# Contiguous feature chunks for the gather, and one-hot slots made one group ahead, in two mixture-of-experts layers

## The chip, the cores and the metric

The kernel runs on one core of one Trainium2 chip. The metric is the device time of one execution, in microseconds (us). A core has five engines that run side by side and wait for each other through semaphores: TensorE (PE; its weight loads are shown apart as PEld), VectorE (DVE), ScalarE (ACT), GpSimd (POOL) and SyncE (SP), which issues nearly all DMAs here.

## What is computed

Two blocks in a row over 256 tokens of 1024 features, in fp32. The change touches only the two mixture-of-experts layers of the second block. Each token picks one group of 8 experts out of 8 groups and two experts inside it, 64 experts in all:

```python
def hier_moe(h, w_grp, b_grp, w_exp, b_exp, w1, w3, w2):
    ...
    g_sel = jnp.argmax(g_logits, axis=-1)
    ...
    top_p, top_i = lax.top_k(e_prob, TOP_K_IN_GROUP)
    gate = g_gate * top_p / jnp.sum(top_p, axis=-1, keepdims=True)
    expert = g_sel[:, None] * EXPERTS_PER_GROUP + top_i
    ...
    def expert_block(args):
        xb, e = args
        hb = jax.nn.silu(xb @ w1[e]) * (xb @ w3[e])
        return hb @ w2[e]
    ...
    y = y_rows[dest].astype(jnp.float32) * gate_sorted[:, None]
    out = jnp.zeros((N, D), jnp.float32).at[tok_sorted].add(y)
```

w1 and w3 are 1024 x 256 per expert, w2 is 256 x 1024. Around each such layer stands x = layer_norm(alpha * x + f). All weights of all 64 experts are read in each layer.

## The kernel before

The first part of the program (two attention layers, an MLP each, then latent attention) ends at about 920 us of the span. Then `moe` runs twice, with a pooling mixer between.

**Tokens and slots.** `moe` goes through 16 groups of four experts, each expert with 32 slots, 128 slots a group. Instead of moving rows, it multiplies: `s1` holds for every token and expert the slot number (or none); a comparison with `iota` makes the one-hot matrix G [128 tokens, 2 blocks, 128 slots] (L1397, VectorE). The **gather** (L1406) multiplies chunks of x with G and gives `xg`, 8 feature chunks by 128 slots, in two halves of four chunks. Gg (L1425, VectorE) is G times the gates; its transpose GT (L1429, evicted at L1431) brings the results back to the tokens.

**Layout of x.** x is [128 tokens, 2 blocks, 1024 features] in SBUF. The expert weights are read so that partition p holds features 8p to 8p + 7, so feature chunk k is k, k + 8, k + 16 and so on:

```python
xk = x.rearrange("p b (q k) -> p b k q", k=8)
```

In the gather a chunk `xk[:, b, k]` is the stationary operand: 128 elements with a step of 8.

**A group on TensorE.** `up` (L1444): 64 matmuls with w1 and w3, 32 columns an expert, four experts in four column strips. ScalarE takes the tanh (L1448), VectorE makes th and h (L1449, L1451). Then `gather(g + 1)`; `back(g + 1)`, the transposes of Gg; `down(g)`: h is transposed (L1459, evicted at L1461), 32 matmuls with w2 (L1470), the eviction to Y (L1474, L1475) and the way back with GT into the sum (L1479). Then `up(g + 1)`. In this program an fp32 matmul leaves two records in the trace, so `up` shows as 128 and a gather as 32. The first seven gathers of a layer are evicted with gain and shift in eight pieces (L1412, L1414); at group GAIN = 6 `affine` (L1068) applies gain and shift to x itself, and alpha times x is added to the sum (L1586). After group OVER = 8 a branch on the device (L1525) handles experts with more than 32 rows; here it is not taken.

**The weights.** They are streamed through a ring of 21 tiles of [128, 2048] fp32, 1.0486 MB each: 10 from a pool that the first part also uses and 11 more. `raw_w(i)` also issues the DMA of item i + 20 (L180, on SP); SP waits there until the tile's earlier user is done. A group takes 8 items of w1 and w3, in pairs, and 4 of w2. The items of the second layer follow those of the first without a break.

**What sets the order.** The schedule is manual: every engine runs its instructions in the order in which the program writes them. PSUM tiles of the experts come in turn from four banks.

Of the kernel before, what the change touches and what calls it, by code (L numbers as in the profile page):

```python
# [70 lines left out]
def _layout(inputs):  # L71
    """The arrays of the launch: the inputs, the small vectors also laid end to end, constants of the shapes."""
    a = {n: np.ascontiguousarray(inputs[n]) for n in _INS}
    a["rows"] = np.concatenate([a[n].reshape(-1, 128) for n in _ROWS])
    a["brows"] = np.concatenate([a[n].reshape(-1, 128) for n in _BROWS])
    a["wr"] = np.concatenate([a["moe_w_grp_2"], a["moe_w_exp_2"]], -1)
    a["br"] = np.concatenate([a["moe_b_grp_2"], a["moe_b_exp_2"]], -1)
    a["cst"], a["poolm"] = _constants()
    return a


class Kern:
# [6 lines left out]
    # ---------------------------------------------------------------- weights  # L89
# [181 lines left out]
    def g_tok(self, xT, key, outs, n, splitn=1, mid=None):  # L271
        """outs[blk][j]: [128, n]: token rows, from both halves of K."""
# [18 lines left out]
    def g_feat(self, xT, key, mid=None, bank=None, end=None):  # L291
        """[128 features, 2, 256 tokens] twice, for 512 features."""
# [73 lines left out]
    def rsqrt(self, r, n):  # L366
        """r <- r ** -0.5 for r [128, n], n <= 4: a seed from the exponent, then Newton steps."""
# [57 lines left out]
    # ---------------------------------------------------------------- attention over pairs of 64-wide heads  # L425
    def attend(self, ap, pairs, scores, V, mask, outp, yts, sink=None, pre=None):
        """Softmax attention, two heads at a time, three pairs in flight. Gives the prologue and the rest."""
# [69 lines left out]
        def main(pend=None, nxt=None, ahead=1):  # L497
            """The pairs in turn; then the products out of the last are still owed. nxt() makes an attention to go on with."""
# [29 lines left out]
    # ---------------------------------------------------------------- mixer 0  # L528
    def mixer0(self):
        nc, A = self.nc, self.A  # L530
        with ExitStack() as st:
# [30 lines left out]
            def lru():  # L562
                col = self.col
                # halves of the biases, 2 * softplus(-lambda)
# [5 lines left out]
                for hf in range(2):  # L570
# [26 lines left out]
                    # tanh(z/2) = w, z = -log a: a = 2/(1+w) - 1, sqrt(1-a^2) = 2 sqrt(w)/(1+w)  # L597
# [34 lines left out]
            def forget():  # L632
                # log sigmoid, running sums, biases
# [72 lines left out]
    def pair_scores(self, qT, kT):  # L706
        """Heads 2p and 2p+1 in the two halves of the partitions of chunk p."""
# [145 lines left out]
    # ---------------------------------------------------------------- squared relu mlp  # L853
# [35 lines left out]
    # ---------------------------------------------------------------- mixer 1  # L889
    def mixer1(self, xT):  # L890
        nc, A = self.nc, self.A
        x = self.x
        with ExitStack() as st:
# [4 lines left out]
            tab = ap.tile([128, 2, 2, 2, 32], F32, name="tab")     # q or k, block, cos or sin  # L898
# [11 lines left out]
            def rope(dst, src, nh, qk, b):  # L910
                """dst, src [128, nh, 64]."""
# [11 lines left out]
            def feat(dst, tk, nch):  # L923
                """tokens x features (two blocks) to features x tokens."""
# [79 lines left out]
    # ---------------------------------------------------------------- rows broadcast to all partitions, layer norm  # L1004
    def bc(self, i, bank=None, mat=None, more=None):
        """row i of brow (times mat's diagonal) on every partition, in two banks; more: rows to add."""
# [10 lines left out]
    def stats(self, y):  # L1017
        """mean and 1 / sqrt(var + eps) of a block of rows in parts, in steps: a seed from the exponent, Newton steps."""
# [23 lines left out]
    def both(self, gens):  # L1042
        """the generators' steps in turn; what they return."""
# [11 lines left out]
    def normed(self, y, dst):  # L1055
        """dst <- (y - mean) / sqrt(var + eps); y[block][half]."""
# [5 lines left out]
    def affine(self, g, bb):  # L1062
        """x <- x * g + b."""
        for o, v in ((ALU.mult, g), (ALU.add, bb)):
            for h in range(2):
                for b in range(2):
                    t = self.x[:, b, h * 512:(h + 1) * 512]
                    self.nc.vector.tensor_tensor(t, t, v[h], op=o)  # L1068

    def router(self, rp):  # L1070
        """the router's weights times the gain of the norm before, less the mean over the rows; its bias plus that of
        the norm's shift. In steps."""
# [22 lines left out]
    def rotary(self):  # L1095
        """tables from the positions: cos, sin [128, block, 16], in steps."""
# [33 lines left out]
    # ---------------------------------------------------------------- latent attention  # L1130
    def mla(self):
        nc, A = self.nc, self.A
        x = self.x
        with ExitStack() as st:
# [33 lines left out]
            # what dies first comes first: the experts' weights follow into it  # L1168
# [97 lines left out]
            # the residual's own norm  # L1266
# [16 lines left out]
    def warm(self, n):  # L1283
        """products that nothing reads, against the drop of TensorE's clock in a wait."""
# [4 lines left out]
    # ---------------------------------------------------------------- experts  # L1289
    def moe(self, l, wp, bank, y, before_last):  # L1290
        """x becomes the norm's output before gain and shift, of y[block][half]; bank: banks that are free at the start.
        The sum is returned. The router's weights are free of their columns' means, so that it can take y as it is."""
# [8 lines left out]
        # logits, token rows; feature chunk k is k, k + 8, ...  # L1301
        xk = x.rearrange("p b (q k) -> p b k q", k=8)
# [4 lines left out]
        for b in range(2):  # L1307
            for h in range(2):
                nc.scalar.activation(x[:, b, h * 512:(h + 1) * 512], y[b][h], AF.Copy)
# [18 lines left out]
        def one_hots(v, n, k):  # L1328
            """the first k of v [128, 2, 8] from the largest on, the first of equals first: one-hot, and values."""
# [32 lines left out]
        def gates():  # L1362
            nonlocal gt, ci
            # gates
# [18 lines left out]
            # further rounds of 32 rows an expert  # L1383
# [10 lines left out]
        def gather(g, s, first=False):  # L1394
            """rows of group g: [128 features, 8, 128 slots], in halves of the features, and the one-hot slots."""
            G = wp.tile([128, 2, 4, 32], F32, name="G", bufs=1)
            tt(G, s[:, :, 4 * g:4 * g + 4, None].to_broadcast([128, 2, 4, 32]),  # L1397
               iota[:, None, None, :].to_broadcast([128, 2, 4, 32]), op=ALU.is_equal)
            Gf = G.rearrange("p b e s -> p b (e s)")
# [20 lines left out]
            return xg, G, half  # L1420

        def back(g, G):
            """the weighted way back [128 slots, 256]."""
            Gg = wp.tile([128, 2, 4, 32], F32, name="Gg", bufs=1)
            tt(Gg, G, gt[:, :, 4 * g:4 * g + 4, None].to_broadcast([128, 2, 4, 32]), op=ALU.mult)  # L1425
# [8 lines left out]
        def up(g, xg, parts, mid=None, fill=()):  # L1434
            """fill: work of others to go between the parts."""
# [18 lines left out]

        def down(g, h, GT, acc, getw2, first, end, fill=()):
            """fill: where the last products are left, if it isn't empty."""
# [4 lines left out]
            nc.scalar.activation(hT, ps, AF.Copy)  # L1461
            if getw2 is None:
# [24 lines left out]
        def last(g, hT, GT, acc):  # L1487
            """the same for the last group, whose weights come in quarters of the columns."""
# [31 lines left out]
        def overflow():  # L1520
            """the experts with more than 32 rows."""
# [3 lines left out]
            with self.tc.If(more > 0):  # L1525
                with self.tc.For_i(0, more, 1):
# [22 lines left out]
                    for g in range(16):  # L1549
                        xg, G, half = gather(g, s2)  # L1550
                        half(1)
                        GT = back(g, G)
                        h = up(g, xg, parts2(g))
                        down(g, h, GT, acc, lambda: getw2(g), False, False)

        xg, G, half = gather(0, s1, True)
        h = up(0, xg, parts(0), lambda: (gates(), half(1)))
        GT = back(0, G)
        acc = self.pacc()
        for g in range(16):  # L1560
            this = h, GT
            w2g = lambda: [((0, 1), [(e, w2(l, g, e)) for e in range(4)])]
            if g == OVER:
                down(g, *this, acc, w2g, False, False)
                overflow()
            if g == GAIN:
                self.affine(self.bc(2 * l), self.bc(4 + 2 * l))
            if g < 15:
                xg, G, half = gather(g + 1, s1, g < GAIN)
                if g:  # L1570
                    half(1)
                    GT = back(g + 1, G)
# [5 lines left out]
            if g != OVER:  # L1578
                down(g, *this, acc, None if (l, g) == (1, 15) else w2g, g == 0, g == 15, fill)
            if g == 0:  # L1580
                half(1)
                GT = back(1, G)
            if g == GAIN:
                for b in range(2):
                    for hf in range(2):
                        nc.tensor.matmul(acc[b][hf], self.alpha_id, x[:, b, hf * 512:(hf + 1) * 512], start=False, stop=False,  # L1586
                                         skip_group_check=True)
            if g < 15:
                h = up(g + 1, xg, parts(g + 1), fill=fill)
        return acc  # L1590

    # ---------------------------------------------------------------- pooling mixer
# [216 lines left out]
```

## Time and profile before

| | us |
|---|---|
| runs of the kernel (device time) | 1928.67, 1929.14, 1932.13; median 1929.14 |
| profiled execution, span from first to last instruction | 1926.0 |
| start of the first expert gather in the span | 920.4 |
| start of the second layer's first gather | 1432.7 |
| end of the last product | 1913.5 |

Start of the reading: the span is one execution, and the device time contains a little around it; the median lies 3.1 us above the span. In the lists, "idle before" is the time for which an engine stood still before an instruction, and behind the arrow stands what ended it. PE records are pipelined and overlap, so their busy time adds up to more than the span they cover. [...] The DMA share is the mean busy share of the core's 16 DMA engines.

### The profile page before, as it was taken

How to read it: one execution, taken by the hardware profiler on the slowest of the kernel's cores; microseconds unless marked ns; L12 is line 12 of the kernel's file. 1: busy time of each engine (PE TensorE's matmuls, PEld its weight loads, DVE VectorE, ACT ScalarE, POOL GpSimd, SP SyncE). 2: the span in 40 equal slices, each digit the busy share in tenths (PEclk: the TensorE clock that was granted, in tenths of full speed). 3: DMA queues.
4: the chain of work that ended last, by engine and by line, in shares of the span. 5: the costliest groups of instructions: out<-in, count | busy, mean ns of one | idle time of the engine just before them, and what ended most of it. 6: DMA issues, size and time to landing. Idle time of an engine off the chain costs nothing. (4 is left out here: it accounts for less than half of the span.)

```text
span 1926.0 us, 29923 instructions
## 1 busy us (share of the span) xinstructions
PE 1748.4 (91%) x12712; PEld 1316.9 (68%) x12712; DVE 749.8 (39%) x1599; ACT 578.8 (30%) x1047; POOL 11.3 (1%) x22
## 2 busy tenths in 40 slices
PE   7999999999999999999888897888998878878886
PEld 7998899989878899877554554555475455545554
DVE  6886576556675655585210111101151111110112
ACT  5644445444564544466111100000021110000001
POOL 0000000000000000000000000000000000000000
PEclk9999999999999999999888889888998879898898
DMA  8544355554524455556899999999989999999993
GB/s 278 179 152 150 117 170 197 187 184 155 196 66 153 147 195 184 177 213 256 341 356 411 415 384 403 409 419 422 418 360 359 378 415 412 386 406 413 422 421 115
DMA packets 160611, 550.11 MB, mean 286 GB/s; under 512 B 9660, under 2 KB 33551, under 8 KB 144463
## 3 DMA queue, kind: packets, MB, share of 16 engines
q1 hardware_dynamic: 158175, 539.18, 73.2%
q0 software_dynamic: 2144, 8.66, 1.2%
q8 instruction: 104, 1.70, 0.3%
q14 instruction: 44, 0.36, 0.0%
q10 hardware_dynamic: 144, 0.21, 0.0%
HBM read 546.97 MB, written 1.05 MB: 285 GB/s over the span
## 5 line engine op out<-in xcount | busy, mean ns | idle before, releaser
L237 DVE TENSOR_TENSOR wl<-wr,wh 128x1024 fp32r<-128x1024 f32 (+4 forms) x268 | 309.5, 1197 | 119.7 <-ACT wh L234 76.1
L1406 PE MATMUL b<-G,x 128*128 128x128 f32 x1024 | 252.5, 418 | 64.6 <-DVE G L1397 64.5
L1406 PEld LDWEIGHTS b<-G,x 128*128 128x128 f32 x1024 | 247.0, 335 | 78.7 <-issue 78.0
L234 ACT ACTIVATE wh<-wr 128x1024 fp32r<-128x1024 f32 (+4 forms) x268 | 265.1, 1037 | 103.9 <-DVE wl L237 72.3
L1444 PE MATMUL b<-wr,xg 128*32 128x256 f32 x4096 | 235.6, 388 | 2.3 <-ACT xg L1414 2.3
L1444 PEld LDWEIGHTS b<-wr,xg 128*32 128x32 f32 x4096 | 129.6, 112 | 113.1 <-issue 28.0
L1470 PE MATMUL b<-wr,hT 128*32 128x512 f32 x992 | 160.6, 806 | 18.0 <-ACT hT L1461 18.0
L320 PE MATMUL a<-wh,yh 128*128 128x512 f32 x416 | 168.0, 404 | 2.7 <-ACT yh L334 2.7
L320 PE MATMUL a<-wh,yl 128*128 128x512 f32 x416 | 165.1, 397 | 0.6 <-DVE yl L335 0.6
L320 PE MATMUL a<-wl,yh 128*128 128x512 f32 x416 | 164.1, 394 | 0.0
L1449 DVE SCALAR_TENSOR_TENSOR th<-th,b 128x256 f32<-128x256 f32 x32 | 13.5, 421 | 326.4 <-ACT th L1448 326.4
L304 PE MATMUL b<-xh,wl 128*128 128x256 f32 x448 | 121.9, 282 | 0.0
L304 PE MATMUL b<-xh,wh 128*128 128x256 f32 x448 | 121.7, 281 | 0.0
L1470 PEld LDWEIGHTS b<-wr,hT 128*32 128x32 f32 x992 | 36.3, 143 | 124.8 <-issue 96.2
L1479 PE MATMUL a<-Y,GT 128*128 128x512 f32 x248 | 118.2, 618 | 0.0
L1448 ACT ACTIVATE th<-b 128x256 f32<-128x256 f32 x32 | 12.3, 384 | 326.9 <-PE b L1444 326.9
L304 PE MATMUL b<-xl,wh 128*128 128x256 f32 x448 | 110.3, 282 | 0.0
L1475 DVE COPY Y<-b 128x512 f32<-128x512 f32 x31 | 21.4, 692 | 206.9 <-PE b L1470 206.9
L320 PEld LDWEIGHTS a<-wh,yh 128*128 128x128 f32 x416 | 78.1, 188 | 23.3 <-ACT yh L334 4.5
L1479 PEld LDWEIGHTS a<-Y,GT 128*128 128x128 f32 x248 | 42.0, 189 | 75.7 <-issue 30.5
L320 PEld LDWEIGHTS a<-wh,yl 128*128 128x128 f32 x416 | 78.1, 188 | 22.5 <-DVE yl L335 3.9
L304 PE MATMUL a<-xh,wh 128*128 128x256 f32 x320 | 90.0, 290 | 1.5 <-ACT xh L348 1.1
(460 smaller groups left out, 2533.2 us busy)
## 6 DMA issues: line engine op xcount, KB each, us to landing
wr<-in_moe_w SPq DMA_DIRECT2D x372, 1024.0 KB, 15.4
wr<-in_mlp_w_up SPq DMA_DIRECT2D x32, 1024.0 KB, 5.3
wr<-in_mlp_w_down SPq DMA_DIRECT2D x32, 1024.0 KB, 4.9
wr<-in_xa_w_kv SPq DMA_DIRECT2D x16, 1024.0 KB, 5.3
wr<-in_xa_w_q SPq DMA_DIRECT2D x8, 1024.0 KB, 4.9
wr<-in_xa_w_o SPq DMA_DIRECT2D x8, 1024.0 KB, 5.0
wr<-in_cd_w_in SPq DMA_DIRECT2D x8, 1024.0 KB, 4.9
wr<-in_moe_w POOLq DMA_DIRECT2D x8, 1024.0 KB, 7.2
```

The lines of the kernel that those rows point to most:

```text
L234: nc.scalar.activation(hi[:, s], r[:, s], AF.Copy)
L237: nc.vector.tensor_tensor(lo[:, s], r[:, s], hi[:, s].bitcast(F32), op=ALU.subtract)
L304: nc.tensor.matmul(o[f // 2][:, f % 2, :], wt[c][:, kk, f * 128:(f + 1) * 128], xT(a, h * 4 + kk), start=(h == 0 and kk == 0 and a == 0 an ...
L320: nc.tensor.matmul(acc[b][hf], yT[a][:, chunk, b * 128:(b + 1) * 128], wt[c][:, j, hf * 512:(hf + 1) * 512], start=(first and a == 0 and c ...
L1406: nc.tensor.matmul(ps[:, k], xk[:, b, 4 * i + k], Gf[:, b], start=(b == 0), stop=(b == 1))
L1444: nc.tensor.matmul(ps[32 * e:32 * e + 32, which], xg[:, k, 32 * e:32 * e + 32], w(e, k), start=(which == 0 and k == 0), stop=(k == 7), ski ...
L1448: nc.scalar.activation(th, ps[:, 0], AF.Tanh, scale=0.5)
L1449: stt(th, th, 1.0, ps[:, 0], op0=ALU.add, op1=ALU.mult)
L1470: nc.tensor.matmul(y[hf][32 * e:32 * e + 32], hT[:, c, 32 * e:32 * e + 32], w(c)[:, hf * 512:(hf + 1) * 512], start=(c == 0), stop=(c == 1 ...
L1475: nc.vector.tensor_copy(Y[:, 512:], y[1])
L1479: nc.tensor.matmul(acc[b][hf], GT[:, b * 128:(b + 1) * 128], Y[:, hf * 512:(hf + 1) * 512], start=first, stop=end, skip_group_check=True)
```

## The change

Three things, all in `moe`:

1. In the expert layers x lies as 8 contiguous chunks of 128 features: `xk` is now a plain slice. Everything that deals in natural feature order goes through a view `xn` with a step of 128 elements between neighbours: the copies into x at the start, `affine`, and the product that adds alpha times x.
2. G and Gg are made by functions of their own (`slots`, `weighted`) and for group g + 2 while group g + 1 is in `up`. After the overflow branch both are made on the spot.
3. The transposes of h (`turned`) are taken out of `down` and stand before those of Gg.

```diff
-        # logits, token rows; feature chunk k is k, k + 8, ...
-        xk = x.rearrange("p b (q k) -> p b k q", k=8)
+        xk = x.rearrange("p b (k q) -> p b k q", k=8)
+        xn = x.rearrange("p b (k q) -> p b q k", k=8)
+        half_x = lambda b, h: xn[:, b, 64 * h:64 * h + 64]
+        by8 = lambda t: t.rearrange("p (q k) -> p q k", k=8)
...
-                nc.scalar.activation(x[:, b, h * 512:(h + 1) * 512], y[b][h], AF.Copy)
+                nc.scalar.activation(half_x(b, h), by8(y[b][h]), AF.Copy)
...
-        def gather(g, s, first=False):
+        def slots(g, s):
             G = wp.tile([128, 2, 4, 32], F32, name="G", bufs=1)
             tt(G, s[:, :, 4 * g:4 * g + 4, None].to_broadcast([128, 2, 4, 32]),
                iota[:, None, None, :].to_broadcast([128, 2, 4, 32]), op=ALU.is_equal)
+            return G
+
+        def weighted(g, G):
+            Gg = wp.tile([128, 2, 4, 32], F32, name="Gg", bufs=1)
+            tt(Gg, G, gt[:, :, 4 * g:4 * g + 4, None].to_broadcast([128, 2, 4, 32]), op=ALU.mult)
+            return Gg
+
+        def gather(G, first=False):
...
         for g in range(16):
-            this = h, GT
...
             if g == OVER:
-                down(g, *this, acc, w2g, False, False)
+                down(g, turned(h), GT, acc, w2g, False, False)
                 overflow()
+                G = slots(g + 1, s1)
+                Gg = weighted(g + 1, G)
             if g == GAIN:
-                self.affine(self.bc(2 * l), self.bc(4 + 2 * l))
+                self.affine(self.bc(2 * l), self.bc(4 + 2 * l), half_x, by8)
+            GTn = None
             if g < 15:
-                xg, G, half = gather(g + 1, s1, g < GAIN)
+                xg, half = gather(G, g < GAIN)
                 if g:
                     half(1)
-                    GT = back(g + 1, G)
+            if g != OVER:
+                hT = turned(h)
+            if 0 < g < 15:
+                GTn = back(Gg)
...
-                        nc.tensor.matmul(acc[b][hf], self.alpha_id, x[:, b, hf * 512:(hf + 1) * 512], start=False, stop=False,
+                        nc.tensor.matmul(acc[b][hf], self.alpha_id, half_x(b, hf), start=False, stop=False,
                                          skip_group_check=True)
+            if g < 14 and g != OVER - 1:
+                G = slots(g + 2, s1)
+                Gg = weighted(g + 2, G)
             if g < 15:
+                GT = GTn
                 h = up(g + 1, xg, parts(g + 1), fill=fill)
```

On TensorE, between the up products of the second and the third group of the first layer, the kernel before has the gather, the transposes of Gg, those of h, the down products and the way back (x16 counts matmuls, keep holds the identity):

```order
L1406 MATMUL b<-G,x 128x128 x16
L1429 MATMUL b<-keep,Gg 128x128 x2
L1459 MATMUL b<-keep,h 128x128 x2
L1470 MATMUL b<-wr_8692,hT 32x512
L1470 MATMUL b<-wr,hT 32x512 x3
```

The same place in the changed kernel:

```order
L1419 MATMUL b<-G,x 128x128 x16
L1469 MATMUL b<-keep,h 128x128 x2
L1440 MATMUL b<-keep,Gg 128x128 x2
L1484 MATMUL b<-wr_8692,hT 32x512
L1484 MATMUL b<-wr,hT 32x512 x3
```

The two pairs of transposes have changed places; the products stand as before.

On VectorE, in the first layer, one group of the kernel before from th of `up` to the eviction of Y (r_s_8831 is the tile of slot numbers s1):

```order
L1449 SCALAR_TENSOR_TENSOR th<-th,b 128x256
L1451 SCALAR_TENSOR_TENSOR h<-th,b 128x128x2
L1397 TENSOR_TENSOR G<-r_s_8831,keep 128x256
L1412 TENSOR_SCALAR xg<-b,pcol 128x128 x4
L1425 TENSOR_TENSOR Gg<-G,r_gt 128x256
L1475 COPY Y<-b 128x512
```

The same group in the changed kernel:

```order
L1460 SCALAR_TENSOR_TENSOR th<-th,b 128x256
L1462 SCALAR_TENSOR_TENSOR h<-th,b 128x128x2
L1425 TENSOR_SCALAR xg<-b,pcol 128x128 x4
L1489 COPY Y<-b 128x512
L1401 TENSOR_TENSOR G<-r_s_8831,keep 128x256
L1407 TENSOR_TENSOR Gg<-G,r_gt 128x256
```

G and Gg moved from between h, the gather's eviction and Y to behind Y, and belong to the group after the next.

## Rows read from the trace of the kernel before

**Rows 1.** The page: the span, and the granted clock in 40 slices of it.

```profile
span 1926.0 us, 29923 instructions
...
PEclk9999999999999999999888889888998879898898
```

**Rows 2.** The timeline of one group; columns: start, us, engine, line, operation, [idle before].

```profile
1760.09 0.40 DVE L1397 TENSOR_TENSOR G<-r_s,keep 128x256 f32<-128x256 f32 x1
...
1760.64 7.86 PE L1406 MATMUL b<-G,x 128*128 128x128 f32 x32 [1.96 <-DVE G L1397]
...
1769.70 0.41 PE L1429 MATMUL b<-keep,Gg 128*128 128x128 f32 x2 [1.21 <-DVE Gg L1425]
...
1770.86 5.24 PE L1470 MATMUL b<-wr,hT 128*32 128x512 f32 x32 [0.53 <-ACT hT L1461]
...
1776.04 3.81 PE L1479 MATMUL a<-Y,GT 128*128 128x512 f32 x8
...
1779.78 7.11 PE L1444 MATMUL b<-wr,xg 128*32 128x256 f32 x128
...
1788.31 0.40 DVE L1397 TENSOR_TENSOR G<-r_s,keep 128x256 f32<-128x256 f32 x1
```

**Rows 3.** The waits from 850 us on: us in total, times, longest us.

```profile
PE b L1406 <- DVE G L1397: 64.5, 30, 5.3
PE b L1429 <- DVE Gg L1425: 53.8, 32, 2.4
```

**Rows 4.** Instructions by line and form, 850 us on: count, busy us, mean ns.

```profile
L1406 PEld LDWEIGHTS b<-G,x 128*128 128x128 f32 x1024 | 247.0, 335 | 78.7 <-issue 78.0 <-PE b L1429 0.3 <-DVE G L1397 0.2
...
L1068 DVE TENSOR_TENSOR x<-x,b 128x512 f32<-128x512 f32 x24 | 14.8, 678 | 3.6 <-PE a L1615 3.2 <-PE a L1618 0.4
...
L1449 DVE SCALAR_TENSOR_TENSOR th<-th,b 128x256 f32<-128x256 f32 x32 | 13.5, 421 | 326.4 <-ACT th L1448 326.4
...
L1451 DVE SCALAR_TENSOR_TENSOR h<-th,b 128x256 f32<-128x256 f32 x32 | 19.2, 599 | 1.1
...
L1618 PEld LDWEIGHTS a<-wr,x 128*128 128x128 f32 x16 | 2.1, 192 | 0.1
```

**Rows 5.** The timeline between the layers: products and transposes with x stationary.

```profile
1408.01 1.05 PE L1618 MATMUL a<-wr,x 128*128 128x128 f32 x8
...
1421.86 2.01 PE L1311 MATMUL a<-keep,x 128*128 128x128 f32 x16
```

**Rows 6.** DMA totals of 930 to 1926, 1780 to 1870 and 1210 to 1350 us.

```profile
DMA packets 88410, 384.10 MB, mean 386 GB/s; under 512 B 5968, under 2 KB 11088, under 8 KB 73168
...
DMA packets 8291, 37.96 MB, mean 422 GB/s; under 512 B 578, under 2 KB 578, under 8 KB 6749
...
DMA packets 12557, 58.39 MB, mean 417 GB/s; under 512 B 889, under 2 KB 889, under 8 KB 9987
```

**Rows 7.** The DMA queue's own waits, 1010 to 1880 us.

```profile
SPq L180 <- PE b L1470: 257.4, 28, 17.5
```

**Rows 8.** The timeline after the branch and between the layers.

```profile
1211.18 8.65 PE L1444 MATMUL b<-wr,xg 128*32 128x256 f32 x128
...
1393.79 3.64 PE L1470 MATMUL b<-wr,hT 128*32 128x512 f32 x32 [0.53 <-ACT hT L1461]
...
1439.43 11.37 SPq L180 DMA_DIRECT2D wr<-in_moe_w  x8
```

**Rows 9.** Stretches: PE, PEld, DVE, ACT, POOL busy us, clock, DMA share, GB/s.

```profile
1430.00:1440.00 10.00, 8.08 (x76) 6.29 (x78) 3.31 (x18) 1.23 (x4) 0.00 (x0) 1.00 0.43 180
1772.00:1774.00 2.00, 2.00 (x12) 0.39 (x8) 0.00 (x0) 0.00 (x0) 0.00 (x0) 0.50 1.00 393
1776.00:1778.00 2.00, 2.00 (x9) 0.81 (x6) 0.69 (x1) 0.00 (x0) 0.00 (x0) 1.00 1.02 418
1888.00:1892.00 4.00, 4.00 (x55) 2.08 (x48) 0.69 (x1) 0.60 (x1) 0.00 (x0) 1.00 0.51 179
```

**Rows 10.** The chain that ended last: the start of its last quarter of products.

```profile
1911.24 1.04 PE b L1500 x16
```

More of the change, by code (lines that the diff above doesn't have):

```diff
@@ L1060, in normed, with affine @@
             nc.vector.tensor_scalar(dst[:, b, 512:], y[b][1], rs, nb, op0=ALU.mult, op1=ALU.add)
-    def affine(self, g, bb):
+    def affine(self, g, bb, half=None, as_=lambda t: t):
+        half = half or (lambda b, h: self.x[:, b, h * 512:(h + 1) * 512])
         for o, v in ((ALU.mult, g), (ALU.add, bb)):
@@ L1066, in affine @@
                 for b in range(2):
-                    t = self.x[:, b, h * 512:(h + 1) * 512]
-                    self.nc.vector.tensor_tensor(t, t, v[h], op=o)
+                    t = half(b, h)
+                    self.nc.vector.tensor_tensor(t, t, as_(v[h]), op=o)
     def router(self, rp):
@@ L1419, in gather, with back @@
             half(0)
[L1420 to L1425, printed above, removed]
+            return xg, half
+        def back(Gg):
             Gg = Gg.rearrange("p b e s -> p b (e s)")
@@ L1453, in up, with turned @@
             return h
-        def down(g, h, GT, acc, getw2, first, end, fill=()):
+        def turned(h):
             ps = self.pb([128, 2, 128])
@@ L1461, in down @@
             nc.scalar.activation(hT, ps, AF.Copy)
+            return hT
+        def down(g, hT, GT, acc, getw2, first, end, fill=()):
             if getw2 is None:
@@ L1549, in overflow, with mid @@
                     for g in range(16):
-                        xg, G, half = gather(g, s2)
+                        G = slots(g, s2)
+                        xg, half = gather(G)
                         half(1)
-                        GT = back(g, G)
+                        GT = back(weighted(g, G))
                         h = up(g, xg, parts2(g))
[L1554 to L1558, printed above, removed]
+                        down(g, turned(h), GT, acc, lambda: getw2(g), False, False)
+        G = slots(0, s1)
+        xg, half = gather(G, True)
+        Gg = []
+        def mid():
+            nonlocal G
+            gates()
+            half(1)
+            Gg.append(weighted(0, G))
+            G = slots(1, s1)
+        h = up(0, xg, parts(0), mid)
+        GT = back(Gg.pop())
+        Gg = weighted(1, G)
         acc = self.pacc()
         for g in range(16):
-            this = h, GT
             w2g = lambda: [((0, 1), [(e, w2(l, g, e)) for e in range(4)])]
             if g == OVER:
-                down(g, *this, acc, w2g, False, False)
+                down(g, turned(h), GT, acc, w2g, False, False)
                 overflow()
+                G = slots(g + 1, s1)
+                Gg = weighted(g + 1, G)
             if g == GAIN:
-                self.affine(self.bc(2 * l), self.bc(4 + 2 * l))
+                self.affine(self.bc(2 * l), self.bc(4 + 2 * l), half_x, by8)
+            GTn = None
             if g < 15:
-                xg, G, half = gather(g + 1, s1, g < GAIN)
+                xg, half = gather(G, g < GAIN)
                 if g:
                     half(1)
-                    GT = back(g + 1, G)
+            if g != OVER:
+                hT = turned(h)
+            if 0 < g < 15:
+                GTn = back(Gg)
             fill = []
@@ L1578, in moe @@
             if g != OVER:
-                down(g, *this, acc, None if (l, g) == (1, 15) else w2g, g == 0, g == 15, fill)
+                down(g, hT, GT, acc, None if (l, g) == (1, 15) else w2g, g == 0, g == 15, fill)
             if g == 0:
                 half(1)
-                GT = back(1, G)
+                GTn = back(Gg)
             if g == GAIN:
```

## Prediction

> **What bounds the kernel now.** The first half of the span (up to about 920 us) is not touched by the change, so I looked for the two expert layers only. The timeline of one group of four experts comes first, since 32 such groups make up nearly all of the second half. Group to group (from one slot comparison G to the next) it takes 1788.31 - 1760.09 = 28.2 us [rows 2]. TensorE works through four blocks in it: the gather L1406 (7.86 us), the down products L1470 (5.24), the way back L1479 (3.81) and the up products L1444 (7.11), and it stands idle 1.96 us before the gather, for G on VectorE, and 1.21 us before the transposes L1429, for Gg. None of the four blocks waits for a weight. The list of waits says the same for all groups: 64.5 us for G and 53.8 us for Gg [rows 3], and no entry of any size that names a load.
>
> The other side is the weight stream. A group needs 12 loads of 1.0486 MB, 12.58 MB. Where the stream is fastest over several groups it moves 421.8 GB/s (37.96 MB in 90 us) [rows 6], which is 12.58 / 0.4218 = 29.8 us a group. That is more than 28.2. So in this stretch TensorE already runs faster than the weights come, and lives on the ring of 21 tiles, which holds 21 x 2.486 = 52.2 us of stream. The DMA queue's own waits show the rest of the picture: 257.4 us of waiting until down products had freed a tile [rows 7]. The stream loses time while the ring is full (43% busy at 1430 to 1440 us [rows 9]) and TensorE then eats the lead. **Both are near their limit, and the change speeds up only one of them.** That decides the size of the gain.
>
> **The change part by part.**
>
> *Contiguous chunks.* A gather is 32 records in 7.86 us [rows 2], 246 ns each, and its weight loads of x take 335 ns [rows 4]. The nearest row with x contiguous as the stationary operand is L1618: 8 records in 1.05 us, 131 ns each [rows 5], with loads of 192 ns [rows 4]. Taken at that, a gather costs 32 x 0.131 = 4.2 us, 3.7 us less. The other bound is no gain at all: the transposes L1311 also load x with the step of 8, and go at 2.01 / 16 = 126 ns [rows 5]. They are transposes, not products, so I take L1618, the same operation, and keep the other as a rival.
> [...]
>
> *What becomes strided instead.* x is now written and read with a step of 128 elements by four ScalarE copies, eight VectorE operations and four products a layer. VectorE's nearest pair is L1449 (421 ns, dense) against L1451 (599 ns, strided output), 256 columns both [rows 4]: 0.18 us per 256, so 0 to 0.36 us on each 512-wide operation now at 678 ns (L1068), 0 to 2.9 us a layer. The four copies, as wide, get at most as much, 1.4 us. The products are bounded by the gather's own 335 / 192 = 1.74, on the 3.81 us that the like eight records of L1479 take [rows 2]: 0 to 2.8 us. I take the upper ends, 7 us a layer on TensorE's side. What hides them is the lead in the ring (below); without it they would cost 14 us in all.
>
> *G and Gg one group ahead.* VectorE makes them during the up products, where it has only th and h to do later. The 1.96 us and 1.21 us go: 3.2 us a group. What is next late on that path is h, which TensorE needs for its own transposes; those now stand behind a gather of 4.2 us, while th and h take 0.42 + 0.60 us on VectorE [rows 4] behind one tanh. Two waits for G stay, one a layer after the overflow branch, where G is made as late as before (up to 5.3 us [rows 3]). Nothing is queued behind G on VectorE that TensorE needs sooner. DMA instructions and their order on SP stay as they are.
>
> *Sum on TensorE.* 28.2 - 3.7 - 3.2 = 21.3 us a group. The clock may add: the down products ran partly at the low level (granted 0.50 at 1772 to 1774 us [rows 9]) right after the idle stretch that goes; at the full level they take 3.64 [rows 8] against 5.24. So 20 to 21.3 us.
>
> *Sum of the stream.* At 21.3 us a group, TensorE eats 8.5 us of lead each group, and the 52.2 us are gone after six groups. From there it waits for weights; the end is set by the stream. After 930 us, when the ring is full and the first tiles are being freed, 384.10 - 1.05 (output) = 383.05 MB are still to come [rows 6]. At 421.8 GB/s this takes 908 us: the last byte lands at 1838. At the 417 GB/s of a longer stretch [rows 6] it is 1849.
> Gaps in the stream: between the layers the ring can fill for 52.2 us. Before, the queue got its first tile of the second layer 1439.43 - 1393.79 = 45.6 us after the last down products began [rows 8]; it becomes 2 us less for the half gather and at most 1.4 us more for the copies. So no gap, where 1430 to 1440 lost 5.7 us. At the affine step the ring is nearly empty and takes the stall. I put 4 us for the start of the first layer and the overflow branch, from 0 to 12: 1842.
> *Tail.* In the profile the last bytes land at about 1889.7 (179 GB/s for 4 us from 1888 [rows 9]) and TensorE is far behind: 36 us to the end. If TensorE waits for weights, only the last quarter is left: from its products at 1911.24 [rows 10] to 1926.0 [rows 1] are 14.8 us, and some 2 us for the quarter before it: 17, from 15 to 21.
> 1842 + 17 = 1859 on the span's scale, 67 us less than 1926.0: 48 from the earlier end of the stream, 19 from the tail. The median of the runs stands 3.1 us above the span (1929.14), so **1862 us**.
>
> **The rivals.**
>
> *The TensorE saving arrives whole.* 32 x 6.9 = 221 us less, less two waits that stay: about 1715. The stream speaks against it: 383 MB in the 770 us left would be 497 GB/s, and no row comes near. 1 in 100.
>
> *The gather stays at 246 ns,* as the transposes L1311 suggest; the change then removes only waits. A group takes 25.0 us, still under 29.8; the lead lasts 52.2 / 4.8 = 11 of 16 groups, and the stream sets the end again, with more small gaps: 1868. 7 in 100.
>
> *The low clock, slower than before.* [...] The row that speaks for it is 0.50 after the idle stretch at 1772 [rows 9]; the clock line of the page has 8 in most slices of the experts, where the first half has 9 [rows 1]. Its price: L1444 after the overflow branch, its first quarter at the low level, took 8.65 us [rows 8] against 7.11 [rows 2], so 1.54 more on 1.78, a factor of 1.87. With a share s of 20.5 us of work at the low level a group takes 20.5 x (1 + 0.87 s): over 29.8 from s = 0.52, and then each microsecond costs 32. It passes 1929 from 31.9 us, s = 0.64; at s = 0.8 the group is 34.8 and the time 2020. Against it: a TensorE that needs over 29.8 us no longer waits, and in the rows the level was back at 1.00 at 1776 to 1778 us, after five microseconds of unbroken work [rows 9]. 4 in 100.
> [...]
>
> *More gaps in the stream.* The strided steps, the affine stall or the branch meet a full ring as at 1430 to 1440 us, 5.7 us each, four or five times: 1885 to 1895. 8 in 100.
>
> **How the numbers follow.** The forecast has 80 in 100, between 1853 (rate 421.8, no gaps, tail 15, first tiles 2 us sooner) and 1884 (rate 417, 12 us of gaps, tail 21). Outside that range lie the whole saving (1), the low clock (4), most of the further gaps (6) and some 6 of my own case. Only the low clock gives slower: 4. Within 0.2% (about what a measurement of this kernel can tell from no change) takes an accident between it and the rest: 1. Faster: 95.
>
> **What would show it.** Gathers of about 4.2 us; no wait of TensorE for G or Gg but the two after the branch; from about the seventh group of each layer waits of TensorE for loads, which the trace of before does not have; groups of 29.8 us there and of 20 to 22 us before; the stream near 421 GB/s from 930 us through the layers' border; last bytes at about 1842 and a tail under 20 us. I am wrong if the stream runs at its rate and the groups are still longer than 29.8 us (then it is the clock or the strided steps), or if the gathers stay at 7.9 us.

## The result and the profile after

The changed kernel takes **1863.08 us** (median of 4 runs, 1862.80 to 1863.42); beside it the kernel before took 1928.91. The ratio is 0.9659, interval 0.9645 to 0.9672: 65.8 us less. The forecast was 1862.0.

Line numbers moved with the edit: the gather is now L1419 (was L1406), G L1401, Gg L1407, the transposes of Gg L1440 and of h L1469, the down products L1484, the way back L1493, `up` L1455, `affine` L1069, the alpha product L1616, the copies into x L1313, the router's transposes L1315, and the last quarters' products L1514.

The page of the changed kernel: span, granted clock, DMA share and rate in 40 slices. PEclk is the clock that TensorE was granted, in tenths of full speed (9 is 90% or more); in the stretches given here it reads as a share instead. In the two traces, of the kernel before and of the changed one, every clock record is at 1.0 or at 0.5, the high and the low level below.

```profile
span 1860.9 us, 29902 instructions
...
PEclk9999999999999999999999989999999998989988
DMA  8543355555534355545899999999999999999996
GB/s 288 182 159 124 126 166 196 186 192 176 181 104 136 114 185 193 188 163 225 304 404 423 421 423 420 422 421 422 418 420 419 421 423 421 423 419 423 421 423 251
```

From slice 22 to 39 the stream runs between 418 and 423 GB/s without a hole. That is new: the page of the kernel before has this line, with 359 to 422 in the same slices.

```profile
GB/s 278 179 152 150 117 170 197 187 184 155 196 66 153 147 195 184 177 213 256 341 356 411 415 384 403 409 419 422 418 360 359 378 415 412 386 406 413 422 421 115
```

The span is 65.1 us shorter than that of [rows 1], and the clock has fewer 8s.

TensorE's timeline of a group early in the first layer, to set against [rows 2]: start, us, line, [idle before].

```profile
954.09 3.84 PE L1419 MATMUL b<-G,x 128*128 128x128 f32 x32
957.77 0.38 PE L1469 MATMUL b<-keep,h 128*128 128x128 f32 x2
957.98 0.38 PE L1440 MATMUL b<-keep,Gg 128*128 128x128 f32 x2
959.69 3.64 PE L1484 MATMUL b<-wr,hT 128*32 128x512 f32 x32 [1.32 <-ACT hT L1471]
963.26 3.81 PE L1493 MATMUL a<-Y,GT 128*128 128x512 f32 x8
966.99 7.11 PE L1455 MATMUL b<-wr,xg 128*32 128x256 f32 x128
974.04 3.84 PE L1419 MATMUL b<-G,x 128*128 128x128 f32 x32
```

The gather has gone from 7.86 to 3.84 us, the waits for G and Gg are gone, and the down products take 3.64 where [rows 2] shows 5.24. Group to group: 974.04 - 954.09 = 19.95 us against 28.2. The only idle time is 1.32 us for hT.

A few groups later, in the same columns, `up` has turned into pieces:

```profile
1009.46 1.92 PE L1455 MATMUL b<-wr,xg 128*32 128x256 f32 x28 [0.22 <-DMA wr<-in_moe_w]
...
1019.42 1.92 PE L1455 MATMUL b<-wr,xg 128*32 128x256 f32 x28 [1.38 <-DMA wr<-in_moe_w]
1021.27 3.84 PE L1419 MATMUL b<-G,x 128*128 128x128 f32 x32
...
1051.06 3.84 PE L1419 MATMUL b<-G,x 128*128 128x128 f32 x32
```

Each of these pieces waits for a load, and the next group takes 1051.06 - 1021.27 = 29.8 us, which is 12.58 MB at 422 GB/s. TensorE is now paced by the stream. The waits from 850 us to the end say so in sum (us, times, longest); they answer [rows 3]:

```profile
PE b L1455 <- DMA wr<-in_moe_w: 86.9, 79, 3.4
...
PE b L1484 <- DMA wr<-in_moe_w: 27.7, 23, 2.9
...
PE b L1419 <- DVE G L1401: 10.5, 4, 4.5
...
PE b L1419 <- DVE x L1069: 8.2, 2, 4.2
```

64.5 us for G became 10.5, in four waits (the first gather and the one after the branch, in each layer); the 53.8 us for Gg are gone; 8.2 us for x behind `affine`, one wait a layer, have come in (in the kernel before, G was made behind `affine` and that gather waited for G); and 114.6 us of waiting for loads have come in, of which the kernel before had none of any size.

### The profile page after: what moved, and what is told of

Its sections match the earlier page's. It is cut to its first block, busy times and chain, and to the rows that moved or that the text cites. A ratio compares the mean times of both kernels' runs of the same rounds, so it can differ in the third digit from the quotient of the medians.

```text
span 1860.9 us, 29902 instructions
## 1 busy us (share of the span) xinstructions
PE 1659.9 (89%) x12712; PEld 1195.0 (64%) x12712; DVE 760.5 (41%) x1599; ACT 577.9 (31%) x1047; POOL 11.2 (1%) x22
## 5 line engine op out<-in xcount | busy, mean ns | idle before, releaser
L1455 PE MATMUL b<-wr,xg 128*32 128x256 f32 x4096 | 287.8, 406 | 89.3 <-DMA wr<-in_moe_w 86.9
L1455 PEld LDWEIGHTS b<-wr,xg 128*32 128x32 f32 x4096 | 137.0, 115 | 244.2 <-DMA wr<-in_moe_w 132.6
L1484 PE MATMUL b<-wr,hT 128*32 128x512 f32 x992 | 151.8, 622 | 50.2 <-DMA wr<-in_moe_w 27.7
L1419 PE MATMUL b<-G,x 128*128 128x128 f32 x1024 | 133.1, 291 | 18.9 <-DVE G L1401 10.5
L1419 PEld LDWEIGHTS b<-G,x 128*128 128x128 f32 x1024 | 126.4, 204 | 33.9 <-issue 18.2
L1484 PEld LDWEIGHTS b<-wr,hT 128*32 128x32 f32 x992 | 34.5, 113 | 146.3 <-issue 59.8
L1493 PE MATMUL a<-Y,GT 128*128 128x512 f32 x248 | 116.1, 610 | 0.0
L304 PE MATMUL a<-xh,wl 128*128 128x256 f32 x320 | 88.8, 286 | 0.9 <-DVE wl L237 0.9
```

Source lines behind the costliest of these rows:

```text
L304: nc.tensor.matmul(o[f // 2][:, f % 2, :], wt[c][:, kk, f * 128:(f + 1) * 128], xT(a, h * 4 + kk), start=(h == 0 and kk == 0 and a == 0 an ...
L1419: nc.tensor.matmul(ps[:, k], xk[:, b, 4 * i + k], Gf[:, b], start=(b == 0), stop=(b == 1))
L1455: nc.tensor.matmul(ps[32 * e:32 * e + 32, which], xg[:, k, 32 * e:32 * e + 32], w(e, k), start=(which == 0 and k == 0), stop=(k == 7), ski ...
L1484: nc.tensor.matmul(y[hf][32 * e:32 * e + 32], hT[:, c, 32 * e:32 * e + 32], w(c)[:, hf * 512:(hf + 1) * 512], start=(c == 0), stop=(c == 1 ...
L1493: nc.tensor.matmul(acc[b][hf], GT[:, b * 128:(b + 1) * 128], Y[:, hf * 512:(hf + 1) * 512], start=first, stop=end, skip_group_check=True)
```

## Experiments

**Each half of the change alone.** The first kernel has the layout and not the order:

```diff
-        xk = x.rearrange("p b (q k) -> p b k q", k=8)
+        xk = x.rearrange("p b (k q) -> p b k q", k=8)
+        xn = x.rearrange("p b (k q) -> p b q k", k=8)
+        half_x = lambda b, h: xn[:, b, 64 * h:64 * h + 64]
+        by8 = lambda t: t.rearrange("p (q k) -> p q k", k=8)
```

> x in contiguous chunks, but G and Gg where the kernel before makes them, and the transposes of h behind those of Gg. Theory (the weight stream sets the end): gathers of 3.8 us, TensorE's group 28.2 - 4.0 = 24 us, still under the stream's 29.8, so nearly the whole gain: 1864 to 1872 us, the last bytes within 5 us of the changed kernel's 1844. Rival (TensorE's chain sets the end, and each saving counts): 32 x 4.0 of the 32 x 8.2 us that the two parts take from TensorE, so half the gain of 66 us: about 1896.

Measured: 1863.09 us, ratio 0.9659 (0.9643 to 0.9675), the whole gain. The second has the order and the old layout; against the changed kernel:

```diff
-        xk = x.rearrange("p b (k q) -> p b k q", k=8)
-        xn = x.rearrange("p b (k q) -> p b q k", k=8)
-        half_x = lambda b, h: xn[:, b, 64 * h:64 * h + 64]
-        by8 = lambda t: t.rearrange("p (q k) -> p q k", k=8)
+        xk = x.rearrange("p b (q k) -> p b k q", k=8)
+        half_x = lambda b, h: x[:, b, h * 512:(h + 1) * 512]
+        by8 = lambda t: t
```

> G and Gg one group ahead and the transposes of h first, but x in the old layout, with its step of 8 in the gather. Theory: gathers stay at 7.9 us, TensorE's group is 28.2 - 3.2 = 25.0 or, with the full clock, 24 us; the stream sets the end: 1864 to 1872. Rival (each saving counts): 32 x 4.2 of 32 x 8.2 us, about 1895. Where both this and the other half alone give nearly all, the two savings don't add.

Measured: 1864.90 us, ratio 0.9671 (0.9654 to 0.9687). So **either half alone gives what both give together**, 64 to 66 us, and both rivals (about 1895) are refuted. The timelines show that each did its own part, and only that: with the layout alone (first fence) the waits for G and Gg stand and the gather is shorter; with the order alone (second fence) the waits are gone and the gather takes what it took.

```profile
1125.76 5.44 PE L1409 MATMUL b<-G,x 128*128 128x128 f32 x32 [1.96 <-DVE G L1400]
1132.41 0.41 PE L1432 MATMUL b<-keep,Gg 128*128 128x128 f32 x2 [1.21 <-DVE Gg L1428]
```

```profile
1115.97 7.89 PE L1418 MATMUL b<-G,x 128*128 128x128 f32 x32
```

A group without waits for weights takes 24.2 us with the layout alone (from 1116.69 to 1140.87 in its timeline), and 22.9 with the order alone (with half of the loads, below, from 1215.19 to 1238.13). Both are under 29.8, and below that more speed on TensorE buys nothing while the stream sets the end.

**Half of the stream.** To see what the two halves are worth without this bound, four kernels and the kernel before read only half of the expert weights: w1 and w3 of the first two experts of a group serve the other two as well, and so with w2, except in the last group. The products are as many and as large as before.

```diff
-                        for q in range(2):
+                        for q in range(1):
...
+                    if (l, g) != (1, 15) and e % 2:
+                        continue
...
-                    w = [self.raw_w(n, l, g, h, q) for q in range(2)]
+                    w = [self.raw_w(n, l, g, h, 0)] * 2
```

The kernel before:

> The kernel before with half of the weight bytes: only one of each two tiles of an expert layer is loaded, and used for both pairs of experts (the last group's w2 is whole). TensorE's work is unchanged; half of the experts are computed with another expert's weights. Theory: TensorE sets the end of the kernel before, so nothing is gained but the stream's share in the tail: 1915 to 1930. Rival (it is already bound by the stream): far less, under 1880.

The changed kernel:

> The changed kernel with half of the weight bytes, in the same way; half of the experts are computed with another expert's weights. Theory: without the stream's bound TensorE's groups of 19.95 us show: 14 groups from the second to the last took 425 us in the kernel before and would take 14 x 20 + 15 for the affine step + 8 for the branch = 303, so 2 x 122 us less than the kernel before: about 1680 us. Rival (the change gives TensorE no more than the 66 us that were measured): about 1860.

The layout alone:

> Contiguous chunks alone, with half of the weight bytes (half of the experts are computed with another expert's weights). Theory (without the stream's bound the parts add): in the run with chunks alone a group without waits for weights took 24.2 us (1116.69 to 1140.87), in the changed kernel with half the bytes 18.9, so 30 x 5.3 = 159 us above that kernel's 1652: about 1811. Rival (one part needs the other, the chunks only pay where the waits for G are gone): 1870 or more.

The order alone:

> G and Gg ahead alone, with half of the weight bytes (half of the experts are computed with another expert's weights). Theory (the parts add): the gather costs 4.0 us more than in the changed kernel, 32 x 4.0 = 129, and the strided steps on x are gone, some 12 us: 1652 + 129 - 12 = 1769. With the other half alone at 1811 the two savings from 1928, 117 and 159, would add up to the 276 of both. Rival (they overlap in time): both alone under 1750.

Both, with the contiguous x that the gather likes taken for every other use as well (the strided view is left out, so the features are mixed up; the work is the same):

> The changed kernel with half of the weight bytes, and with the copies into x, the affine step and the alpha product on x as dense operations (features end up in another order than the weights want, and half of the experts use another expert's weights). It prices the strided steps where no stream hides them. Theory, from the trace of the changed kernel: affine 7.47 instead of 4.85 us, the alpha product 7.07 instead of 3.60, the copies about 1 us, twice: 1652 - 14 = 1638. Rival (VectorE and the product hide each other): 1650.

| half of the loads | us | ratio | interval |
|---|---|---|---|
| before | 1927.88 | 0.9990 | 0.9976 to 1.0004 |
| layout alone | 1796.05 | 0.9314 | 0.9276 to 0.9353 |
| order alone | 1764.66 | 0.9152 | 0.9118 to 0.9185 |
| changed kernel | 1651.78 | 0.8563 | 0.8546 to 0.8580 |
| changed, no strided use | 1631.70 | 0.8462 | 0.8429 to 0.8495 |

Four things follow. The kernel before does not mind half of its loads: the chain through TensorE, its waits for VectorE included, set its time. Without the bound the layout is worth 1928 - 1796 = 132 us, the order 163, both 276, so of the change's 276 us the stream lets 66 through. The strided steps cost 1651.78 - 1631.70 = 20 us (two runs of each kernel; the spans of the two profiles differ by 17.9), which the full stream hides. And the two parts together give a little less than their sum of 295. The last four came out 4 to 28 us below what was expected of them (1811, 1769, 1680 and 1638), and every rival named with them is refuted.

The group of the changed kernel with half of the loads, TensorE's timeline:

```profile
1184.04 7.11 PE L1457 MATMUL b<-wr,xg 128*32 128x256 f32 x128
1191.09 3.84 PE L1421 MATMUL b<-G,x 128*128 128x128 f32 x32
...
1195.68 3.64 PE L1486 MATMUL b<-wr,hT 128*32 128x512 f32 x32 [0.31 <-ACT hT L1473]
...
1202.93 1.29 PE L1457 MATMUL b<-wr,xg 128*32 128x256 f32 x20
```

That is 1202.93 - 1184.04 = 18.9 us, where the prediction had 20 to 21.3. TensorE's granted clock also differs. The clock lines of the pages, the kernel before with half of the loads first, the changed kernel with half of the loads behind it:

```profile
PEclk9999999999999999999888889888898889888888
```

```profile
PEclk9999999999999999999999999999999999999999
```

With no shortage of weights in either, the 8s of [rows 1] go away with the change. The order alone also has 9 in every slice; the layout alone, with the two waits a group still there, keeps four 8s. The mean granted clock of the profiled runs is 0.934 before, 0.967 with the layout alone, 0.986 with the order alone and 0.992 with both. So most of the low level went with the two waits, but the shorter gather alone also took some of it.

**The step of the stationary operand.** The changed kernel, but the gather in iteration g of the loop takes x with a step of 1, 2, 4 or 8 elements, in turn (it reads all of x, and other features make up a chunk than should):

```diff
-                        nc.tensor.matmul(ps[:, k], xk[:, b, 4 * i + k], Gf[:, b], start=(b == 0), stop=(b == 1))
+                        nc.tensor.matmul(ps[:, k], chunk(b, 4 * i + k), Gf[:, b], start=(b == 0), stop=(b == 1))
...
-                xg, half = gather(G, g < GAIN)
+                xg, half = gather(G, g < GAIN, (1, 2, 4, 8)[g % 4])
```

> The changed kernel, whose gathers read x with a step of 1, 2, 4 or 8 elements in turn, by group (the rows are then multiplied in another order of the features than the weights want). [...] Rival (any step costs, or in proportion): step 2 near 5, step 4 near 7.9. The total stays within 1860 to 1868, since the stream sets the end.

Measured, timeline of four gathers in a row: steps of 2, 4, 8 and 1.

```profile
953.70 4.04 PE L1420 MATMUL b<-G,x 128*128 128x128 f32 x32
...
973.84 7.73 PE L1420 MATMUL b<-G,x 128*128 128x128 f32 x32
...
997.68 7.89 PE L1420 MATMUL b<-G,x 128*128 128x128 f32 x32
...
1021.67 3.84 PE L1420 MATMUL b<-G,x 128*128 128x128 f32 x32
```

A step of 2 costs 5%, a step of 4 nearly all of what a step of 8 costs; the mean weight load is 192, 196, 328 and 334 ns for 1, 2, 4 and 8. So the edge lies between 2 and 4 elements (8 and 16 bytes). The author's own estimate had a step of 4 at the 3.84 us of a step of 1, and the rival had 2 near 5 us: each was wrong on one step. Why the edge lies there no run shows. The time of the whole, 1862.59 us in one run, did not move: every second gather 4 us longer, and the stream hides it.

**The end of the stream.** In the changed kernel the rate falls at the end: windows with PE, PEld, DVE, ACT, POOL busy us, clock, DMA share, GB/s.

```profile
1826.00:1843.00 17.00, 15.29 (x154) 7.77 (x146) 1.03 (x2) 2.73 (x6) 0.00 (x0) 1.00 0.93 329
1843.00:1846.00 3.00, 3.00 (x24) 1.68 (x24) 1.14 (x4) 0.38 (x1) 0.00 (x0) 1.00 0.14 50
```

The last group's w2 comes in 8 loads of 512 KB with runs of 1 KB. One kernel takes 4 loads of 1 MB with runs of 2 KB there; the unaltered kernel ran beside it.

```diff
-                                   [:, :, :, e * 256:(e + 1) * 256], (2, 4, 256)))
+                                   [:, e % 2, :, i * 512:(i + 1) * 512], (4, 512)))
```

> The changed kernel whole, but the last group's w2 comes as 4 loads of 1 MB whose runs are 2 KB long, where it came as 8 loads of 512 KB with runs of 1 KB; the products, the evictions and the writes of that group go by halves with it. Theory (the stream slows at its end because of the short runs): from 1826 us on the changed kernel moved 277 to 372 GB/s, where 421 was usual; at full rate the last bytes land about 3 to 5 us earlier, the larger last piece costs about 0.8 us more after the landing, so about 1860 us (1859 to 1862), and no window of 5 us before the last landing under 400 GB/s. Rival (the rate at the end falls because only a few transfers are left in flight, whatever their runs): the same fall in the last windows, 1863 to 1865 us.

> The changed kernel unaltered, beside the one with the larger last loads on the same chip: 1863 us, its stream's end again at 277 to 372 GB/s.

Measured: 1862.91 us (ratio 0.9656, 0.9642 to 0.9669) against 1862.10 (0.9655, 0.9641 to 0.9670) for the unaltered kernel, whose end ran at 295 to 352 GB/s in windows of 5 us from 1825 to 1840: no gain. The windows of the one with the larger loads, and the step of its chain of work (what the end hung on, followed back) that ends with the last of them:

```profile
1826.00:1839.20 13.20, 12.30 (x118) 6.10 (x106) 1.03 (x2) 1.86 (x5) 0.00 (x0) 1.00 0.99 374
1839.00:1845.00 6.00, 4.91 (x32) 2.01 (x32) 0.42 (x1) 0.77 (x2) 0.00 (x0) 1.00 0.29 113
```

```profile
1831.85 13.15 DMA wr<-in_moe_w
```

The rate did rise, from 329 to 374 GB/s, but not to 421, and windows of 5 us under 400 remain (396, 349, 361), where none was expected; and then it fell to 113 for the last 6 us (share 0.29), in which the last load, issued at 1831.85, landed, 13.15 us after its issue. For the first 7 of these the engines were still busy with earlier loads (0.99), and from issue to landing the median load of the changed kernel takes 19.4 us, so the length of that step by itself says nothing. Both of the reasons in the expectation may act; what part each has stays open.

The chain of the unaltered changed kernel shows why there was little to win:

```profile
1817.14 18.23 DMA wr<-in_moe_w
...
1835.42 1.92 PE b L1455 x28
...
1846.12 1.05 PE b L1514 x16
```

The last load that its end hung on is one of `up`, landed at 1835.4. From there TensorE has work of its own until the last quarter, which starts at 1846.12, and waits for no w2 load by more than half a microsecond. Loads of w2 that land sooner don't shorten that.

## Why the prediction came out right

**The bound.** Right, and half of it could have been said more sharply. The text called both TensorE and the stream near their limit. The half stream shows that TensorE, with its waits for VectorE, set the time before (0.9990), and the timeline after shows that the stream sets it now, from the fifth group of a layer on.

**The gather.** 3.84 us against 4.2, 120 ns a record against the 131 of [rows 5]. L1618 was the right row, the same operation with the same layout; eight records make a rougher mean than 32. The rival "the gather stays" is refuted. Its time was not far off, though: the order alone, with gathers of 7.89 us, took 1864.90, inside the stated range, so the total by itself does not test this step. The row that spoke for it, the transposes, is no counterexample: by form, count, busy us and mean ns, they go after the change at

```profile
L1315 PE MATMUL a<-keep,x 128*128 128x128 f32 x16 | 2.1, 276 | 1.1 <-ACT x L1313 1.1
L1315 PEld LDWEIGHTS a<-keep,x 128*128 128x128 f32 x16 | 1.8, 140 | 1.9 <-ACT x L1313 1.4 <-issue 0.5
```

276 ns, where the kernel before has 279 (L1311), while their loads went from 193 to 140. So the step of 8 cost their loads time too, but not their pace, 126 ns a record before.

**What became strided.** Mis-sized, from below. By form, these are rows of the kernel before, and behind them those of the changed kernel (for `affine` of 1083 to 1092 us alone, its eight operations in the first layer; the line also serves eight dense ones between the layers):

```profile
L1586 PE MATMUL a<-x,keep 128*128 128x512 f32 x16 | 7.2, 592 | 0.0
...
L1309 ACT ACTIVATE x<-a 128x512 f32<-128x512 f32 x4 | 2.4, 598 | 1.4 <-PE a L320 1.1
```

```profile
L1069 DVE TENSOR_TENSOR x<-x,b 128x512 f32<-128x512 f32 x8 | 7.5, 1013 | 0.0
```

```profile
L1616 PE MATMUL a<-x,keep 128*128 128x512 f32 x16 | 14.1, 1038 | 0.0
...
L1313 ACT ACTIVATE x<-a 128x512 f32<-128x512 f32 x4 | 3.8, 1099 | 1.1 <-PE a L320 1.1
```

An `affine` operation went from 678 to 1013 ns, 0.34 us more, just inside the stated 0 to 0.36; the eight took 7.47 us instead of 4.85. The alpha product, 592 ns a record before, takes 1038: eight records in 7.07 us instead of 3.60, so 3.5 us a layer where the upper end was 2.8. The step that failed is the factor of 1.74, the ratio of two durations of loads. The record's duration did grow by about that (1038 / 592 = 1.75), but records overlap, and what counts is their pace: 3.60 / 8 = 450 ns became 7.07 / 8 = 884, a factor of 1.96. The gathers say the same, 246 to 120 ns, 2.05; the pace of [rows 2] and [rows 5] would have given 1.88. The copies cost 0.5 us each (598 to 1099), 1.9 us a layer against at most 1.4. These parts are 2.6 + 3.5 + 1.9 = 8.0 us a layer, 16 in all, where the text had 14. What reaches TensorE without the stream's cover is another sum, and it has a term that the text put at nothing: what the longer `affine` does to the gather behind it. With half of the loads, the gather behind `affine` and the alpha product in the first layer, the changed kernel first and the one without strided use behind it:

```profile
1060.53 5.71 PE L1421 MATMUL b<-G,x 128*128 128x128 f32 x32 [4.21 <-DVE x L1071]
...
1074.15 7.07 PE L1622 MATMUL a<-x,keep 128*128 128x512 f32 x8
```

```profile
1057.10 4.21 PE L1421 MATMUL b<-G,x 128*128 128x128 f32 x32 [0.73 <-DVE x L1071]
...
1069.22 3.60 PE L1622 MATMUL a<-x,keep 128*128 128x512 f32 x8
```

TensorE waits 3.5 us longer for x, and the gather itself takes 1.5 us longer (3.1 in the second layer). With the alpha product that is 8.4 us in the first layer and 10.0 in the second, together about the 17.9 us between the two spans; the other stretches differ by less than 3 us, both ways. With all loads, the changed kernel's gather behind `affine` runs its first 3.31 of 6.99 us at a granted clock of 0.50 (last section, second window). The 18 us did no harm because the ring covered it, as the text said, and the half stream shows the cover gone.

**G and Gg.** Right in the main: 118.3 us of waits became 10.5, and 8.2 with another name, for x behind `affine`. The text spoke of two waits that stay; there are four for G, with those at the start of a layer, and these two.

**The clock.** It was put down as something that "may add" 1.3 us; it came, 3.64 for the down products. Together with it the group went to 19.95 early in a layer and to 18.9 later, with half of the loads, so the text's 20 to 21.3 was too long. The lead also ended sooner: the first wait for a load is in `up` of the fifth group, at 1009 us, not in the seventh. At 29.8 - 19.95 = 9.85 us a group, four groups ate some 40 us, so by this estimate TensorE did not begin with the 52.2 us of a full ring. Neither moved the end, since the stream had it from there on.

**The stream.** DMA totals of 1000 to 1840 us, in the columns of [rows 6]:

```profile
DMA packets 80336, 352.41 MB, mean 420 GB/s; under 512 B 5415, under 2 KB 9348, under 8 KB 66441
```

420 against 421.8, and no gap at the layers' border (417 to 424 GB/s in each window of 20 us from 1350 to 1430). The last bytes came between 1843 and 1846 (50 GB/s there), say 1844.5, instead of 1842: 1826 to 1843 at 329 GB/s moved 17 x (0.421 - 0.329) = 1.6 MB less than the full rate would, 3.7 us. About the 4 us put down for gaps were spent, but there, at a place that the text did not name.

**The tail.** 1860.9 - 1844.5 = 16.4 us against 17, and from the last quarter's products it is 1860.9 - 1846.1 = 14.8, as stated. The path is another one, though, so some of this is luck. The text had TensorE waiting for the last quarters of w2; by the chain above, the end left the stream at 1835.4 and hung on 25.5 us of work behind it, and the last bytes of w2 came about when TensorE was ready for them.

**The rivals.** The saving did not arrive whole (1863, not 1715), but the half stream shows what it would be. The low clock did not decide. The stretch that most looks like it, in the timeline and as a window:

```profile
1800.76 3.64 PE L1455 MATMUL b<-wr,xg 128*32 128x256 f32 x32 [3.39 <-DMA wr<-in_moe_w]
1805.66 3.63 PE L1455 MATMUL b<-wr,xg 128*32 128x256 f32 x28 [1.26 <-DMA wr<-in_moe_w]
```

```profile
1805.66:1809.22 3.56, 3.56 (x29) 1.36 (x29) 0.00 (x0) 0.00 (x0) 0.00 (x0) 0.50 1.01 422
930.00:1840.00 910.00, 746.62 (x6726) 390.76 (x6726) 153.92 (x356) 100.21 (x221) 0.00 (x0) 0.95 1.02 419
```

Behind waits of 3.39 and 1.26 us, 28 records took 3.63 us at 0.50, where the 28 at 1019.42, above, take 1.92 at 1.00. But over the whole stretch the mean is 0.95, higher than the 8s of [rows 1], and the stream kept 422 GB/s in that piece and 419 over the stretch, so the low level cost nothing there: the time comes out of a wait.

The low level does not follow every wait for a load: the piece at 1805.66 ran at 0.50 behind a wait of 1.26 us, but the one at 1019.42, at 1.00 behind 1.38. Which waits are followed by the low level these rows don't settle.

Two sums of the text are slightly off: the terms of its lower end add up to 1854, not 1853, and the chances inside and outside the range to 97 in 100.

The prediction was right because its end did not hang on the size of TensorE's saving. On TensorE's side the sizes were off by up to 40% (the strided steps, 14 against 20 us), and none of these errors reached the total; the three terms that did (bytes over rate, gaps, tail) were within 4 us each, the last two by a path that the text did not have.

## What to carry to other kernels

Put the time that a group needs on the engine beside the time that its bytes need at the best rate the trace shows; once an edit has the first below the second, further savings on the engine are worth nothing, and the end is bytes over rate plus the tail. Halving the loads, in the kernel before as in the kernel after, tells in two runs who holds the end and what an edit would be worth without the other bound. When a layout is turned round, price the uses that become strided by the operand that they are on, with what waits behind them, and look for the work that hides them.

## What the hardware showed that was not expected

- The step of the fp32 stationary operand had an edge, not a slope: the 32 records of a gather take 3.84, 4.04, 7.73 and 7.89 us with steps of 1, 2, 4 and 8 elements.
- A strided moving operand cost as well: with a step of 128 elements, eight records of 512 columns take 7.07 us instead of 3.60.
- The strided gather hardly felt the clock, the contiguous one does. In the kernel before, all 28 whole gathers take 7.85 to 7.89 us, also where the granted clock was 0.50 for the first half (first window below, behind the overflow branch of the first layer: 7.89). In the changed kernel the gather behind `affine`, in the second window, took 6.99 instead of 3.84. With the layout alone, whose gathers still stand behind a wait of 1.96 us or so, the one at 1125.76 takes 5.44 us (granted 0.61 in its first half, 0.77 in its second), and all 32 take 151.4 us by line, 4.73 each, so others are shorter; which of them are, behind the same wait, these rows don't settle.

```profile
1201.59:1205.50 3.91, 3.91 (x16) 3.91 (x17) 0.00 (x0) 0.00 (x0) 0.00 (x0) 0.50 1.03 417
```

```profile
1090.19:1093.50 3.31, 3.17 (x13) 2.88 (x14) 0.88 (x1) 0.00 (x0) 0.00 (x0) 0.50 1.03 418
```

- The stream slows at its end: 329 GB/s from 1826 to 1843 in the changed kernel, and with larger last loads 374 and then 113, where 420 was usual. Why is not shown.
